# One Hyena layer with a SwiGLU feed-forward on one core: the element work of GpSimd goes to VectorE, and parts of VectorE's work go to ScalarE and to adding DMAs

## The chip, the core and the metric

The kernel runs on one core of one Trainium2 chip. The metric is the time of one execution on the device, in microseconds. A core has TensorE (PE in the profile: matmuls, and PEld for their weight loads), VectorE (DVE), ScalarE (ACT), GpSimd (POOL) and SyncE (SP). Each engine works through its own list of instructions in a fixed order; semaphores are all that ties the lists together. DMAs are issued here by SyncE (plain loads and stores) and by GpSimd (DMAs that add what they carry to what stands at the destination, and some stores).

## The reference

The model has one layer: `x + hyena(rmsnorm(x))`, then `x + swiglu(rmsnorm(x))`, then a last rmsnorm. Sequence and width are both 1024, the feed-forward is 2816 wide, all in float32. The mixer is what matters here:

```python
z = short_conv(u @ w_in + b_in, conv_w, conv_b)     # width 3, per channel
x0, x1, v = jnp.split(z, 3, axis=-1)
s = v * x1
g = hyena_filter(L, ...)                            # (2L, D), made by a small MLP
g = g / jnp.sum(jnp.abs(g), axis=0, keepdims=True)
y = irfft(rfft(s, n=2*L, axis=0) * rfft(g, n=2*L, axis=0), n=2*L, axis=0)[:L]
y = (y + s * skip) * x0
return y @ w_out + b_out
```

## The kernel before

The 1024 channels are cut into eight blocks of 128 (i = 0 to 7). Channels lie along the partitions for the projections, and the 1024 positions along the free dimension, in the order "residue mod 8, then the rest". The work runs in this order.

**Prologue.** rmsnorm and transposes of x, the MLP of the filter, and the projections of block 0.

**Hyena blocks**, the loop at line 483. For each block:

- `inproj` (L111, tiles `z`) makes one projection of 128 channels: 48 matmuls of 512 columns, because each float32 product is made of three products of a high and a low part. A block needs three: v, x1 and x0. `load_w_in` makes the low part of a weight with `split_dma`: ScalarE writes the high part (L120) and its negative (L121), and GpSimd issues a DMA that adds the raw weight (L122).
- `short_conv` (L310) takes a projection from PSUM to SBUF with the width-3 convolution: one ScalarE pass (L312), four VectorE passes that multiply and add (L319: two of 896 columns, two of 127) and a VectorE add of two columns for the edges (L320).
- `conv_vx` multiplies v and x1 to the signal s (L417, on GpSimd).
- `filter_g` makes the filter's taps (`ph` matmuls, `hw`), their L1 norm (L395, one VectorE reduction over absolute values) and their spectrum `gg`. `forward` transposes s (`pst`), and makes its spectrum `ss` (`pp` matmuls). Both end in `from_psum` (L360 ScalarE, L361 and L362 VectorE) and `butterfly` (L336 to L352): a small FFT of twelve additions and two multiply-adds. The butterfly of `gg` runs on GpSimd except for L352, that of `ss` on VectorE.
- `pointwise` multiplies the two spectra (L446 to L449 on GpSimd, L450 on VectorE; all on VectorE for block 7). `inverse` (L454, L455 and a butterfly, on VectorE) makes `vv`, and `finish` the result: `py` matmuls, L470 (ScalarE), L471 (VectorE) and the product with x0 (L472, on GpSimd for blocks 0 to 5), then a store to DRAM.

The blocks are run into one another: while block i is finished, the filter, the projections and the forward transform of block i+1 are under way. A scheduler of the framework fixes the order on each engine from its own estimate of times; the source's order gives priorities only. PSUM has two tiles `mm` (projections) and two tiles `cv` (all others). Tiles of SBUF are named by slot: `gg0` and `gg1` hold the filter's spectrum in turn, `ss` and `cr` the signal's spectrum and products, `ct_g` and `ct_d` the scratch of the two butterflies.

**Output projection** (`po`, L566), rmsnorm, and then the **feed-forward**: gate and up products (L714) and the down product (L944), both by a seven-product scheme for 2x2 blocks. In these stages the change edits nothing.

Of the kernel before, what the change touches and what calls it, by code (L numbers as in the profile page):

```python
# [73 lines left out]
def hyena_ffn_kernel(ctx: ExitStack, tc: tile.TileContext, a: dict, out: bass.AP):  # L74
# [280 lines left out]

    def from_psum(pts, E, o, nm):
        av, bv = ab_tiles(E, nm)
        for r in range(2):
# [2 lines left out]
            V.tensor_tensor(ar, pts[r][:, 0:512], br, ALU.add)  # L361
            V.tensor_tensor(br, pts[r][:, 0:512], br, ALU.subtract)  # L362
        butterfly(E, av, bv, o, nm)

    last_load = [None]

    def filter_g(i):
# [27 lines left out]
        V.tensor_reduce(  # L395
            l1, hw.rearrange("p j h c -> p c (j h)"), AX.X, ALU.add, apply_absolute_value=True
        )
        pts = []
        for r in range(2):
# [6 lines left out]
            pts.append(pt)  # L406
        gg = slot(f"gg{i % 2}", f"gg{i}", (2, NB, P))
        from_psum(pts, G, gg, f"g{i}")
        return gg, l1

    def conv_vx(i, pv, px):
        vz = slot("vz", f"vz{i}")
        short_conv(pv, vz, 16 + i)
# [4 lines left out]
        return s

    def conv_x0(i):  # L420
        x0 = slot("x0" if i < NB - 1 else "vz", f"x0{i}")
        short_conv(inproj(i), x0, i)
        return x0

    def forward(i, s):
        pst = cv_psum(f"pst{i}")
        for j in range(NB):
            T.transpose(pst[:, j * P : (j + 1) * P], s[:, j * P : (j + 1) * P], ident)
# [1 line left out]
        S.copy(sT.rearrange("p j c -> p (j c)"), pst)  # L430
        pts = []
        for r in range(2):
            pt = cv_psum(f"pp{i}_{r}")
            for j in range(NB):
                T.matmul(
                    pt[:, j * P : (j + 1) * P], fwd[r][:, j, :], sT[:, j, :], start=True, stop=True
                )
# [4 lines left out]

    def pointwise(i, ss, gg):
        cr = slot("cr" if i < NB - 1 else "ss", f"cr{i}", (2, NB, P))
        E = G if i < NB - 1 else V
        E.tensor_tensor(cr[:, 0], ss[:, 0], gg[:, 1], ALU.mult)  # L446
# [1 line left out]
        E.tensor_tensor(gg, ss, gg, ALU.mult)
        E.tensor_tensor(ss[:, 0], cr[:, 0], cr[:, 1], ALU.add)  # L449
        V.tensor_tensor(ss[:, 1], gg[:, 0], gg[:, 1], ALU.subtract)  # L450

    def inverse(i, ss):
# [1 line left out]
        V.tensor_tensor(av, ss[:, :, 0:4], ss[:, :, 4:8], ALU.add)  # L454
# [4 lines left out]

    def finish(i, vv, s, l1, x0):  # L460
# [10 lines left out]
        V.scalar_tensor_tensor(s, py, rn, s, ALU.mult, ALU.add)  # L471
# [598 lines left out]
```

## Time and profile before

| what | value |
|---|---|
| runs | 1278.81, 1277.39, 1271.57 us; median 1277.39 |
| the profiled execution | 1272.72 us, of which the span of instructions is 1271.0 us |
| TensorE busy in the span | 1181.9 us (93%) |
| VectorE | 922.4 us (73%) |
| ScalarE | 459.4 us (36%) |
| GpSimd | 334.1 us (26%) |
| mean granted TensorE clock | 0.976 |

The same execution by stage (busy us of each engine; the first column is the stretch in us from the span's start):

| stretch | what runs there | TensorE | VectorE | ScalarE | GpSimd |
|---|---|---|---|---|---|
| 0 to 40 | loads, norm, transposes | 18.77 | 23.43 | 23.88 | 3.07 |
| 40 to 120 | first projections, MLP of the filter | 77.72 | 42.58 | 35.33 | 18.94 |
| 120 to 480 | Hyena blocks | 325.03 | 343.74 | 114.76 | 219.50 |
| 480 to 560 | end of block 7, output projection | 75.51 | 48.86 | 32.32 | 8.79 |
| 560 to 640 | output projection, norm, first gate products | 70.86 | 57.78 | 35.76 | 24.39 |
| 640 to 1020 | gate and up products | 379.43 | 242.34 | 114.02 | 38.76 |
| 1020 to 1080 | turn to the down product | 52.17 | 35.42 | 18.90 | 4.24 |
| 1080 to 1271 | down product, last norm | 182.43 | 128.21 | 84.49 | 16.44 |

A row of the profile's timeline reads: start in us, length in us, engine, line, operation, tile written <- tiles read, shapes, count, and in brackets how long the engine had been idle and what ended that. A row of the groups by line reads: line, engine, operation, names, shapes, count | busy us, mean ns of one | idle time before them and what ended it. A row of the waits reads: who <- for whom: us in total, times, longest. A row of the stretches gives busy us and count for PE, PEld, DVE, ACT and POOL, then the granted TensorE clock, the share of the DMA engines and GB/s.

### The profile page before, as it was taken

The numbers are of one execution on the slowest core, as the hardware profiler recorded it, in microseconds if no ns is written. First come the engines' busy times: TensorE is split into PE (matmuls) and PEld (weight loads), VectorE is DVE, ScalarE is ACT, GpSimd is POOL, SyncE is SP. The second block draws the span as 40 slices with busy tenths as digits, with TensorE's granted clock in tenths as the row PEclk, the third lists the DMA queues.
The fourth block names the chain that finished last, engine by engine and source line by source line (L and its number), as shares of the span: only waits on it lengthen the run. The fifth ranks groups of instructions, "written<-read, shape, count | busy, mean of one in ns | idle before, by whom it ended". The sixth has DMA issues, their size and how long they took to land.

```text
span 1271.0 us, 15010 instructions
## 1 busy us (share of the span) xinstructions
PE 1181.9 (93%) x5678; PEld 979.9 (77%) x5678; DVE 922.4 (73%) x1363; ACT 459.4 (36%) x718; POOL 334.1 (26%) x322
## 2 busy tenths in 40 slices
PE   3899978799899798998899999999999998999997
PEld 3678867788788687876678888888888876888885
DVE  6555999899999999456865676666666647955675
ACT  6435323324143134434423332323332323334444
POOL 0024666548646652113310111100111110011100
PEclk9999989999899999999899999999999998999999
DMA  9635545222222329822131332322323259833333
GB/s 282 150 89 120 124 87 137 59 62 63 67 61 73 100 83 274 240 78 72 58 103 57 123 116 92 124 93 75 122 89 119 75 176 342 317 100 91 92 92 132
DMA packets 93993, 152.82 MB, mean 120 GB/s; under 512 B 7135, under 2 KB 58463, under 8 KB 93793
## 3 DMA queue, kind: packets, MB, share of 16 engines
q1 hardware_dynamic: 76241, 91.30, 21.8%
q0 software_dynamic: 17680, 60.57, 18.6%
q8 instruction: 44, 0.72, 0.2%
q14 instruction: 28, 0.23, 0.1%
HBM read 102.30 MB, written 40.11 MB: 112 GB/s over the span
## 4 chain that ended last, share of the span: by engine, by line
PE 63%; DVE 25%; DMA 6%; ACT 3%; issue 2%; POOL 1%; SPq 0%; ACTq 0%; DVEq 0%; POOLq 0%
PE bx L944 9%; PE z L111 7%; PE po L566 5%; PE by L944 5%; PE bz L944 2%; DVE l L395 2%; DVE ss L450 1%; DMA dc<-in_hy_decay_dram 1%; DVE vz L319 1%; DVE fwl L378 1%; DMA xt<-in_x_dram 1%; PE wu3dc L714 1%; PE wg1dc L714 1%; PE wu8dc L714 1%; PE wg5dc L714 1%
## 5 line engine op out<-in xcount | busy, mean ns | idle before, releaser
L111 PE MATMUL z<-uh,whl 128*128 128x512 f32 x768 | 222.4, 403 | 7.9 <-DVE x L319 2.8
L111 PEld LDWEIGHTS z<-uh,whl 128*128 128x128 f32 x768 | 145.5, 192 | 40.7 <-ACT uh L100 3.1
L111 PE MATMUL z<-ul,whl 128*128 128x512 f32 x384 | 128.8, 405 | 0.0
L944 PE MATMUL bx<-wop,hop 128*128 128x512 f32 x504 | 120.2, 399 | 5.6 <-ACT wop L100 4.0
L944 PEld LDWEIGHTS bx<-wop,hop 128*128 128x128 f32 x504 | 96.5, 192 | 28.2 <-ACT wop L100 4.5
L561 POOL DMA_DIRECT2D hd<-g x40 | 21.6, 542 | 330.6 <-DVE g L860 167.2
L566 PE MATMUL po<-wohl,uh 128*128 128x512 f32 x256 | 83.4, 408 | 6.6 <-ACT uh L100 3.7
L101 DVE TENSOR_TENSOR hop<-hrp,hop 128x1024 fp32r<-128x1024 f32 (+1 forms) x41 | 46.3, 1130 | 54.6 <-ACT hop L100 54.6
L111 PEld LDWEIGHTS z<-ul,whl 128*128 128x128 f32 x384 | 73.6, 193 | 15.6 <-issue 0.5
L100 ACT CAST hop<-hrp 128x1024 fp32r<-128x1024 f32 (+1 forms) x41 | 40.0, 977 | 104.3 <-PE bx L944 62.0
L561 POOL DMA_DIRECT2D hrp<-hd x42 | 22.3, 530 | 195.4 <-DVE hop L101 181.8
L566 PEld LDWEIGHTS po<-wohl,uh 128*128 128x128 f32 x256 | 49.0, 194 | 19.3 <-ACT uh L100 4.2
L944 PE MATMUL by<-wop,hop 128*128 128x512 f32 x264 | 60.8, 391 | 0.0
L944 PEld LDWEIGHTS by<-wop,hop 128*128 128x128 f32 x264 | 49.6, 188 | 10.9
L405 PE MATMUL pg<-hw,fwd 128*128 128x128 f32 x256 | 49.6, 277 | 7.9 <-DVE hw L393 7.2
L101 DVE TENSOR_TENSOR wop<-wd,wop 128x512 fp32r<-128x512 f32 x75 | 49.3, 684 | 4.5 <-ACT wop L100 4.5
L566 PE MATMUL po<-wohl,ul 128*128 128x512 f32 x128 | 51.4, 406 | 0.0
L404 PE MATMUL pg<-hw,fwd 128*128 128x128 f32 x256 | 49.7, 276 | 0.0
L100 ACT CAST wop<-wd 128x512 fp32r<-128x512 f32 x75 | 43.2, 616 | 14.7 <-PE by L944 11.9
L122 POOL DMA_DIRECT2D whl<-wt x24 | 22.5, 937 | 98.6 <-ACT whl L121 87.2
L405 PEld LDWEIGHTS pg<-hw,fwd 128*128 128x128 f32 x256 | 39.4, 193 | 8.8 <-DVE hw L393 7.4
L120 ACT CAST whl<-wt 128x1024 fp32r<-128x1024 f32 x24 | 25.0, 1043 | 49.8 <-DMA wt<-in_hy_w_in_dram 26.8
(1720 smaller groups left out, 2968.5 us busy)
## 6 DMA issues: line engine op xcount, KB each, us to landing
hrp<-hd POOLq DMA_DIRECT2D x35, 512.0 KB, 3.9
wt<-in_hy_w_in_dram SPq DMA_DIRECT2D x24, 512.0 KB
whl<-wt POOLq DMA_DIRECT2D x24, 512.0 KB, 4.6
wgr<-in_ffn_w_gate_dram SPq DMA_DIRECT2D x22, 512.0 KB
wur<-in_ffn_w_up_dram SPq DMA_DIRECT2D x22, 512.0 KB
wd<-in_ffn_w_down_dram SPq DMA_DIRECT2D x44, 256.0 KB
hd<-g POOLq DMA_DIRECT2D x40, 256.0 KB, 2.7
hd<-sx POOLq DMA_DIRECT2D x30, 256.0 KB, 2.8
```

The lines of the kernel that those rows point to most:

```text
L100: S.copy(hi, src)
L101: (eng or V).tensor_tensor(lo, src, hi.bitcast(F32), ALU.subtract)
L111: T.matmul(pt[:, h * 512 : (h + 1) * 512], w[wi], u2[ui][h][:, k, :], start=first and ti == 0, stop=last and ti == len(TERMS) - 1,)
L120: S.copy(hi, src)
L122: G.dma_start(lo.bitcast(F32), src, accum_op=ALU.add)
L395: V.tensor_reduce(l1, hw.rearrange("p j h c -> p c (j h)"), AX.X, ALU.add, apply_absolute_value=True)
L404: T.matmul(o, fwd[r][:, j, :], hw[:, j, 0, :], start=True, stop=False)
L405: T.matmul(o, fwd[2 * r][:, jj, :], hw[:, jj, 1, :], start=False, stop=True)
L561: G.dma_start(dst, src)
L566: T.matmul(o, u2[yi][th][:, k, m * P : (m + 1) * P], wos[h][k // 2][wi][:, k % 2, :], start=(k == 0 and ti == 0), stop=(k == NB - 1 and ti ...
L714: T.matmul(pt, t[:, wi, k, :], b(k)[ui], start=first and k == 0 and ti == 0, stop=k == 3 and ti == len(TERMS) - 1, skip_group_check=not first,
L944: T.matmul(pt, ho[hi_][:, x, q * P : (q + 1) * P], wo_[wi][:, x, :], start=fresh and first and x == 0 and ti == 0, stop=last and x == n - ...
```

## The change

In the Hyena blocks:

- **No element work on GpSimd.** The butterfly of `gg`, the product s, the products of the spectra and the product with x0 all go to VectorE. GpSimd only issues DMAs there.
- **Short convolution of v, and of x0 for blocks 0 to 5**: `short_conv_dma`. ScalarE writes the middle tap to z and the two other taps to a tile `taps` (six passes more, two of them of one column), and two GpSimd DMAs add `taps` to z. x1, and x0 of blocks 6 and 7, keep `short_conv`.
- **Pointwise product.** VectorE writes both products with the real part at once (L466, 2048 columns, one operand read twice by a stride of zero), then two products of 1024 columns into `ss` (L467, L468, one with a factor of -1). A GpSimd DMA of 1 MB adds `ss` to `cr` (L470); for block 7 VectorE adds. The result is now `cr`.
- **L1 norm**: ScalarE takes absolute values in three passes, VectorE adds in five steps, in place of one reduction.
- **Low part of the filter's weights** (`fwl`): by `split_dma` in place of a VectorE subtraction.
- **One spectrum buffer**: `gg` always lies in `gg0`; `gg1` holds `taps`. The slots of `ss` and `cr` swap for blocks 6 and 7.

```diff
+    def short_conv_dma(pt, z, n):
+        w0, w1_, w2_ = (cols[:, 24 + 24 * i + n : 25 + 24 * i + n] for i in range(3))
+        taps = slot("gg1", f"taps{n}", (2, 1024))
+        S.activation(z, pt, AF.Identity, bias=beta[:, n : n + 1], scale=w1_)
+        S.activation(taps[:, 0, 128:1024], pt[:, 0:896], AF.Copy, scale=w0)
+        S.activation(taps[:, 0, 1:128], pt[:, 896:1023], AF.Copy, scale=w0)
+        S.copy(taps[:, 0, 0:1], edge[:, n, 0:1])
+        G.dma_start(z, taps[:, 0], accum_op=ALU.add)
+        S.activation(taps[:, 1, 0:896], pt[:, 128:1024], AF.Copy, scale=w2_)
+        S.activation(taps[:, 1, 896:1023], pt[:, 1:128], AF.Copy, scale=w2_)
+        S.copy(taps[:, 1, 1023:1024], edge[:, n, 1:2])
+        G.dma_start(z, taps[:, 1], accum_op=ALU.add)
...
-    def butterfly(E, av, bv, o, nm, packed=False):
+    def butterfly(av, bv, o, nm, packed=False):
+        E = V
...
-        S.copy(fwh, fw)
-        V.tensor_tensor(fwl, fw, fwh.bitcast(F32), ALU.subtract)
+        split_dma(fwh, fwl, fw)
...
-        V.tensor_reduce(
-            l1, hw.rearrange("p j h c -> p c (j h)"), AX.X, ALU.add, apply_absolute_value=True
-        )
+        ma = slot("ct_g", f"ma{i}")
+        hf = hw.rearrange("p j h c -> p (j h c)")
+        S.activation(ma, hf[:, 0:1024], AF.Abs)
+        V.tensor_tensor(ma[:, 0:512], ma[:, 0:512], ma[:, 512:1024], ALU.add)
+        for q in (2, 3):
+            S.activation(ma[:, 512:1024], hf[:, q * 512 : (q + 1) * 512], AF.Abs)
+            V.tensor_tensor(ma[:, 0:512], ma[:, 0:512], ma[:, 512:1024], ALU.add)
+        V.tensor_tensor(ma[:, 0:256], ma[:, 0:256], ma[:, 256:512], ALU.add)
+        V.tensor_tensor(l1, ma[:, 0:128], ma[:, 128:256], ALU.add)
...
-        gg = slot(f"gg{i % 2}", f"gg{i}", (2, NB, P))
-        from_psum(pts, G, gg, f"g{i}")
+        gg = slot("gg0", f"gg{i}", (2, NB, P))
+        from_psum(pts, "ab_g", gg, f"g{i}")
...
-        short_conv(pv, vz, 16 + i)
+        short_conv_dma(pv, vz, 16 + i)
...
-        G.tensor_tensor(s, vz, xz, ALU.mult)
+        V.tensor_tensor(s, vz, xz, ALU.mult)
...
-        short_conv(inproj(i), x0, i)
+        (short_conv_dma if i < NB - 2 else short_conv)(inproj(i), x0, i)
...
-        E = G if i < NB - 1 else V
-        E.tensor_tensor(cr[:, 0], ss[:, 0], gg[:, 1], ALU.mult)
-        E.tensor_tensor(cr[:, 1], ss[:, 1], gg[:, 0], ALU.mult)
-        E.tensor_tensor(gg, ss, gg, ALU.mult)
-        E.tensor_tensor(ss[:, 0], cr[:, 0], cr[:, 1], ALU.add)
-        V.tensor_tensor(ss[:, 1], gg[:, 0], gg[:, 1], ALU.subtract)
+        V.tensor_tensor(cr, ss[:, 0:1].broadcast_to([P, 2, NB, P]), gg[:, ::-1], ALU.mult)
+        V.tensor_tensor(ss[:, 0], ss[:, 1], gg[:, 0], ALU.mult)
+        V.scalar_tensor_tensor(ss[:, 1], ss[:, 1], -1.0, gg[:, 1], ALU.mult, ALU.mult)
+        if i < NB - 1:
+            G.dma_start(cr, ss, accum_op=ALU.add)
+        else:
+            V.tensor_tensor(cr, cr, ss, ALU.add)
+        return cr
...
-        (G if i < NB - 2 else V).tensor_tensor(s, s, x0, ALU.mult)
+        V.tensor_tensor(s, s, x0, ALU.mult)
```

Lines up to 320 keep their numbers; later ones are higher in the changed kernel (L454 becomes L477, L361 becomes L375). `taps` is one slot for v and x0, so ScalarE's writes to it wait until the adds of the taps before have landed. The edits also make the scheduler place instructions anew, in the Hyena blocks above all.

GpSimd's order around the products of block 5, before (`ss5`, `gg5`, `cr5` are the spectra of block 5, `sig4` is s of block 4, `g6` the butterfly of the next filter, `whl` the weights of a projection):

```order
L446 TENSOR_TENSOR cr5_2590<-ss5_2542,gg5_2298 128x1024 [waits DVE_49,PE_49,Pool_49]
L447 TENSOR_TENSOR cr5_2590<-ss5_2542,gg5_2298 128x1024
L472 TENSOR_TENSOR sig4_2056<-sig4_2056,x04_2451 128x1024 [waits DVE_49]
L448 TENSOR_TENSOR gg5_2298<-ss5_2542,gg5_2298 128x2048 [waits Pool_49]
L122 DMA whl23_3086<-wt23_3084 128x1024 [waits DMASW2_49,DMAHW5_49,PE_49,Activation_49]
L449 TENSOR_TENSOR ss5_2542<-cr5_2590 128x1024 [waits Pool_49]
L417 TENSOR_TENSOR sig6_2838<-vz6_2824,xz6_2831 128x1024 [waits DMAHW6_49,DVE_49]
L336 TENSOR_TENSOR g6ct_2699<-g6ab_2692 128x512 [waits DVE_49]
```

And now (DMASW names the semaphore of a DMA that GpSimd issued):

```order
L333 DMA x04_2540<-taps4_2596 128x1024 [waits DMASW2_49]
L329 DMA vz6_2925<-taps22_2926 128x1024 [waits DMASW6_49,DVE_49,Activation_49]
L333 DMA vz6_2925<-taps22_2926 128x1024 [waits DMASW6_49,Activation_49]
L122 DMA whl5_2948<-wt5_2946 128x1024 [waits DMASW0_49,DMAHW4_49,PE_49,Activation_49]
L122 DMA whl23_3203<-wt23_3201 128x1024 [waits DMASW1_49,DMAHW5_49,PE_49,Activation_49]
L122 DMA whl15_3258<-wt15_3256 128x1024 [waits DMASW0_49,DMAHW6_49,PE_49,Activation_49]
L329 DMA x05_2945<-taps5_3001 128x1024 [waits DMASW3_49,DMASW5_49,DVE_49,Activation_49]
L470 DMA cr5_2683<-ss5_2635 128x2048 [waits DMASW4_49,DVE_49]
L333 DMA x05_2945<-taps5_3001 128x1024 [waits DMASW3_49,Activation_49]
```

The element work is gone from GpSimd's list, and the low parts of the weights (L122) stand behind the tap adds, of which the second (L333) waits for the first (L329) to land.

VectorE's order from the products to the inverse transform of block 4, before:

```order
L450 TENSOR_TENSOR ss4_2149<-gg4_1905 128x1024 [waits Pool_49]
L361 TENSOR_TENSOR g5ab_2299<-pg5_0_2264,g5ab_2299 128x512 [waits Activation_49]
L362 TENSOR_TENSOR g5ab_2299<-pg5_0_2264,g5ab_2299 128x512 [waits DVE_49]
L454 TENSOR_TENSOR y4ab_2203<-ss4_2149 128x1024 [waits Pool_49]
L455 TENSOR_TENSOR y4ab_2203<-ss4_2149 128x1024
```

And now the same place of block 5 (`ma6` is the L1 norm of the next filter, `sig6` the next s, `hw6` the next taps):

```order
L466 TENSOR_TENSOR cr5_2683<-ss5_2635,gg5_2383 128x2048 [waits DVE_49]
L495 TENSOR_TENSOR sig4_2129<-sig4_2129,x04_2540 128x1024 [waits DMASW5_49,DVE_49]
L406 MEMSET hw6_2718 1x128 [waits DVE_49]
L467 TENSOR_TENSOR ss5_2635<-ss5_2635,gg5_2383 128x1024 [waits DVE_49]
L405 TENSOR_TENSOR hw6_2718<-ph6_1_2737,hw6_2718 128x1024 [waits PE_49]
L468 SCALAR_TENSOR_TENSOR ss5_2635<-ss5_2635,gg5_2383 128x1024 [waits DVE_49]
L436 TENSOR_TENSOR sig6_2943<-vz6_2925,xz6_2936 128x1024 [waits DMAHW7_49,DMASW7_49]
L411 TENSOR_TENSOR ma6_2749<-ma6_2749 128x512 [waits Activation_49]
L414 TENSOR_TENSOR ma6_2749<-ma6_2749 128x512 [waits Activation_49] x2
L415 TENSOR_TENSOR ma6_2749<-ma6_2749 128x256 [waits DVE_49]
L477 TENSOR_TENSOR y5ab_2688<-cr5_2683 128x1024 [waits DMASW4_49]
L478 TENSOR_TENSOR y5ab_2688<-cr5_2683 128x1024
```

Between the last product (L468), which lets the 1 MB add go, and L477, which waits for that add, stand five VectorE instructions.

More of the change, by code (lines that the diff above doesn't have):

```diff
@@ L320, in short_conv, with ab_tiles @@
         V.tensor_tensor(z[:, 0:1024:1023], z[:, 0:1024:1023], edge[:, n, :], ALU.add)
-    def ab_tiles(E, nm):
-        ab = slot("ab_g" if E is G else "ab_d", nm + "ab", (2, 2, 4, P))
+    def short_conv_dma(pt, z, n):
[10 more added lines that the diff above has]
+        G.dma_start(z, taps[:, 1], accum_op=ALU.add)
+    def ab_tiles(which, nm):
+        ab = slot(which, nm + "ab", (2, 2, 4, P))
         return ab[:, 0], ab[:, 1]
-    def butterfly(E, av, bv, o, nm, packed=False):
+    def butterfly(av, bv, o, nm, packed=False):
+        E = V
         a23 = av[:, :, 3:1:-1] if packed else av[:, :, 2:4]
@@ L332, in butterfly @@
         bf = bv.rearrange("p r q c -> p (r q) c")
-        ct = slot("ct_g" if E is G else "ct_d", nm + "ct", (8, P))
+        ct = slot("ct_d", nm + "ct", (8, P))
         cc = ct[:, 0:4].rearrange("p (r q) c -> p r q c", r=2)
@@ L354, in butterfly, with from_psum @@
             )
-    def from_psum(pts, E, o, nm):
-        av, bv = ab_tiles(E, nm)
+    def from_psum(pts, which, o, nm):
+        av, bv = ab_tiles(which, nm)
         for r in range(2):
@@ L362, in from_psum @@
             V.tensor_tensor(br, pts[r][:, 0:512], br, ALU.subtract)
-        butterfly(E, av, bv, o, nm)
+        butterfly(av, bv, o, nm)
     last_load = [None]
@@ L421, in conv_x0 @@
         x0 = slot("x0" if i < NB - 1 else "vz", f"x0{i}")
-        short_conv(inproj(i), x0, i)
+        (short_conv_dma if i < NB - 2 else short_conv)(inproj(i), x0, i)
         return x0
+    SPEC = [("ss", "cr")] * (NB - 2) + [("cr", "ss"), ("hw", "ss")]
     def forward(i, s):
@@ L438, in forward @@
             pts.append(pt)
-        ss = slot("ss" if i < NB - 1 else "hw", f"ss{i}", (2, NB, P))
-        from_psum(pts, V, ss, f"s{i}")
+        ss = slot(SPEC[i][0], f"ss{i}", (2, NB, P))
+        from_psum(pts, "ab_d", ss, f"s{i}")
         return ss
     def pointwise(i, ss, gg):
-        cr = slot("cr" if i < NB - 1 else "ss", f"cr{i}", (2, NB, P))
-        E = G if i < NB - 1 else V
-        E.tensor_tensor(cr[:, 0], ss[:, 0], gg[:, 1], ALU.mult)
-        E.tensor_tensor(cr[:, 1], ss[:, 1], gg[:, 0], ALU.mult)
-        E.tensor_tensor(gg, ss, gg, ALU.mult)
-        E.tensor_tensor(ss[:, 0], cr[:, 0], cr[:, 1], ALU.add)
-        V.tensor_tensor(ss[:, 1], gg[:, 0], gg[:, 1], ALU.subtract)
+        cr = slot(SPEC[i][1], f"cr{i}", (2, NB, P))
+        V.tensor_tensor(cr, ss[:, 0:1].broadcast_to([P, 2, NB, P]), gg[:, ::-1], ALU.mult)
[6 more added lines that the diff above has]
+        return cr
     def inverse(i, ss):
-        av, bv = ab_tiles(V, f"y{i}")
+        av, bv = ab_tiles("ab_d", f"y{i}")
         V.tensor_tensor(av, ss[:, :, 0:4], ss[:, :, 4:8], ALU.add)
         V.tensor_tensor(bv, ss[:, :, 0:4], ss[:, :, 4:8], ALU.subtract)
-        vv = slot("cr" if i < NB - 1 else "ss", f"vv{i}", (2, NB, P))
-        butterfly(V, av, bv, vv, f"y{i}", packed=True)
+        vv = slot(SPEC[i][0], f"vv{i}", (2, NB, P))
+        butterfly(av, bv, vv, f"y{i}", packed=True)
         return vv
@@ L480, in hyena_ffn_kernel @@
     ss = forward(0, s)
-    pointwise(0, ss, gg)
+    ss = pointwise(0, ss, gg)
     vv = inverse(0, ss)
@@ L492, in hyena_ffn_kernel @@
             ss1 = forward(i + 1, s1)
-            pointwise(i + 1, ss1, gg)
+            ss1 = pointwise(i + 1, ss1, gg)
         x0 = conv_x0(i)
@@ L500, in hyena_ffn_kernel @@
         if not last:
-            pointwise(i + 1, ss1, gg)
+            ss1 = pointwise(i + 1, ss1, gg)
         if i < NB - 3 or last:
```

## Prediction

> **What bounds the kernel now.** I read the stretches first, then what TensorE waits for, then single instructions on VectorE and GpSimd. The stretch of the Hyena blocks:
>
> ```profile
> 120.00:480.00 360.00, 325.03 (x1910) 284.55 (x1910) 343.74 (x428) 114.76 (x164) 219.50 (x152) 0.96 0.35 85
> ```
>
> TensorE is idle 35.0 of 360 us, its granted clock is 0.96, and VectorE is busy for 95% of the time; in the table by stage, the gate and up products leave TensorE idle for 0.6 of 380 us. The waits of TensorE in that stretch, the longest:
>
> ```profile
> PE pg L405 <- DVE hw L393: 7.2, 1, 7.2
> PE pst L428 <- DVE g3ab L362: 6.6, 1, 6.6
> PE pn L462 <- DVE s1ab L362: 5.9, 1, 5.9
> PE pn L462 <- DVE s4ab L362: 4.2, 1, 4.2
> PE pn L462 <- DVE s2ab L362: 4.1, 1, 4.1
> ```
>
> 28.0 of the 35.0 us, all on VectorE: it is late, and TensorE, with work for most of the time, stands behind it. Why VectorE is so full is seen in its own rows, here beside one of GpSimd (timeline; the first is GpSimd's):
>
> ```profile
> 141.16 4.82 POOL L448 TENSOR_TENSOR gg<-ss,gg 128x2048 f32<-128x2048 f32 x1
> ```
> ```profile
> 142.67 3.34 DVE L320 TENSOR_TENSOR xz<-xz,edge 128x2 f32<-128x2 f32 x1
> 150.79 1.82 DVE L454 TENSOR_TENSOR y0ab<-ss 128x1024 f32<-128x1024 f32 x1
> 165.92 1.29 DVE L352 SCALAR_TENSOR_TENSOR vv<-y0ab 128x512 f32<-128x512 f32 x2
> 499.63 0.15 DVE L320 TENSOR_TENSOR x<-x,edge 128x2 f32<-128x2 f32 x1
> 506.63 1.22 DVE L454 TENSOR_TENSOR y7ab<-ss 128x1024 f32<-128x1024 f32 x1
> 509.51 0.41 DVE L338 TENSOR_TENSOR y7ct<-y7ab 128x256 f32<-128x256 f32 x1
> 513.58 1.29 DVE L352 SCALAR_TENSOR_TENSOR vv<-y7ab 128x512 f32<-128x512 f32 x2
> ```
>
> An add of two columns takes 0.15 us alone, and 3.34 us when it starts inside GpSimd's L448: it ends when that ends (141.16 + 4.82 = 145.98; 142.67 + 3.34 = 146.01). The inverse transform of block 0, beside GpSimd's butterfly, takes 165.92 + 1.29 - 150.79 = 16.4 us; that of block 7, when GpSimd has no element work, 8.2 us (506.63 to 514.87), instruction for instruction the same. So much of VectorE's time is waiting inside its instructions for GpSimd.
>
> **The length of a block.** The transposed signal is copied once a block:
>
> ```profile
> L430 ACT COPY sT<-pst x8: 989/1002/1017, 115.2 to 469.0; 128x1024 f32<-128x1024 f32 x8
> ```
>
> (469.0 - 115.2) / 7 = 50.5 us a block; the stretch of 360 us holds 7.1. Per block VectorE is busy 343.74 / 7.1 = 48.2 us, TensorE 45.6 us, of which up to 0.04 x 50.5 = 2.0 are its slower clock.
>
> **VectorE after, per block.** Its operations at their lengths without GpSimd's element work:
>
> ```profile
> 102.91 2.96 DVE L319 SCALAR_TENSOR_TENSOR x<-z,cols,x 128x896 f32<-128x896 f32 x4
> 131.80 2.34 DVE L392 TENSOR_TENSOR hw<-ph,hw 128x1024 f32<-128x1024 f32 x2
> 182.83 3.77 DVE L395 TENSOR_REDUCE l<-hw 128x128 f32<-128x2048 f32 x1
> 482.39 0.68 DVE L361 TENSOR_TENSOR s7ab<-pp,s7ab 128x512 f32<-128x512 f32 x1
> 493.68 1.27 DVE L471 SCALAR_TENSOR_TENSOR sig<-py,rn,sig 128x1024 f32<-128x1024 f32 x1
> 496.76 1.22 DVE L446 TENSOR_TENSOR cr<-ss,gg 128x1024 f32<-128x1024 f32 x1
> 500.84 2.28 DVE L448 TENSOR_TENSOR gg<-ss,gg 128x2048 f32<-128x2048 f32 x1
> ```
>
> The inverse of 8.2 us begins with two additions of 1.1 (1.22, but instructions overlap by some 0.08), so a butterfly with its two multiply-adds is 6.0 us; the four PSUM adds (L361's kind) are 0.6 each. So: s 8.4, filter spectrum 8.4 (before 2.4 + 1.3, the rest on GpSimd), inverse 8.2, one short convolution 3.1 (before three, 9.3), taps 2.5, L1 norm 3 x 0.6 + 0.6 = 2.4 (before 3.8), products of the spectra 2.28 + 1.22 + 1.27 = 4.8 (before 1.2), s product, L471 and x0 product 1.22 + 1.27 + 1.22 and a reciprocal = 3.9 (before 1.4), low part of the filter weights none (before 0.4). Sum after 41.7. The same sum before is 38.9, against 48.2 busy: 9.3 us a block go in waits for GpSimd, some 66 us in the stretch. The change adds 2.8 us of work to VectorE and takes those 9.3 away: 48.2 to 41.7.
>
> **What the new waits cost.** VectorE now stands in its list at L477 until the 1 MB add has landed. From issue to landing, by the DMA groups:
>
> ```profile
> whl<-wt POOLq DMA_DIRECT2D x24, 512.0 KB, 4.6
> ...
> hd<-g POOLq DMA_DIRECT2D x40, 256.0 KB, 2.7
> ...
> hrp<-hd POOLq DMA_DIRECT2D x35, 512.0 KB, 3.9
> ...
> ul<-yr POOLq DMA_DIRECT2D x6, 256.0 KB, 10.0
> ```
>
> `whl` is the same kind, an add from SBUF to SBUF. 1 MB is not in the trace. Below it is bounded by 4.6; above by 10.0, adds of 256 KB that were issued in a crowd. From 256 to 512 KB is 1.2 us, so I take 4.6 + 2.4 = 7.0, near the lower end, since these adds stand apart from each other. Between L468 and L477 VectorE has five instructions, 1.2 + 3 x 0.6 + 0.3 = 3.3 us: it stalls 3.7 us a block, between 1.3 and 6.7. Behind L477 stands the inverse and then the filter's butterfly; for `py`, which reads the inverse's `vv`, TensorE has from `pg` on 88 projection matmuls, `pst` and `pp` to do first, 25 us at the rates below, so 3.7 us there cost nothing but VectorE's own time. VectorE's block: 41.7 + 3.7 = 45.4.
>
> The tap adds are in series: 2.7 us of ScalarE (1.2 and 1.4, rows below), 4.6, then 4.6 again: v is ready 12 us after its projection, x0 too. s is needed a whole block later, x0 as well: nothing on the path. Behind the second tap add stands `whl` of the x0 projection; it lands some 13 us after v's projection ends. TensorE comes to it after 48 matmuls of x1 (less those done), `pst` and `pp`:
>
> ```profile
> 155.02 3.73 PE L435 MATMUL pp<-sT,fwd 128*128 128x128 f32 x32
> ...
> 158.82 1.09 PE L111 MATMUL z<-uh,whl 128*128 128x512 f32 x4
> ```
>
> 48 x 0.229 + 0.9 + 3.6 = 15.5 us: 2.5 us to spare. If that is gone, TensorE waits for the excess in each block.
>
> ScalarE has 114.76 / 7.1 = 16.1 us a block. It gains two sets of taps and absolute values:
>
> ```profile
> L121 ACT ACTIVATE whl<-whl 128x1024 fp32r<-128x1024 f32 x17 | 18.0, 1057 | 0.4
> ...
> L312 ACT ACTIVATE vz<-z,beta,cols 128x1024 f32<-128x1024 f32 x6 | 7.2, 1199 | 3.5 <-PE z L111 3.5
> ```
>
> At about 1.0 for 896 columns, 0.3 for 127, 0.2 for one, two taps are 3.0, twice 6.0; absolute values 1.1 + 2 x 0.6; 0.4 for `fwl`: 8.7 us, to 25 of some 46. It hides, and it now frees the PSUM of v and x0 itself, without VectorE. The single `gg` buffer costs nothing: VectorE reads it in L468 and writes it later in the same list. `fwl` is added 20 us ahead of its matmuls.
>
> **A rule against the change.** GpSimd's issue beside VectorE's additions of SBUF data:
>
> ```profile
> 278.75 0.87 POOL L122 DMA_DIRECT2D whl<-wt  x1 [8.46 <-ACT whl L121]
> 278.95 0.41 DVE L346 TENSOR_TENSOR ss<-s3ct 128x256 f32<-128x256 f32 x1
> ```
>
> Beside the issue the addition of 256 columns takes the 0.41 us that it takes alone (509.51, above), so I add nothing for the six issues more a block. The Trainium skill, "SBUF — State Buffer", section "SBUF: two separate sides", warns that a DMA issued by GpSimd stalls while VectorE runs an operation that holds both its port pairs, since GpSimd cannot write the descriptors; the rows above do not show it for these additions. If it held here, an issue could wait for the longest of them, 2.28 us, and the landing be 6.9 in place of 4.6: the case of the half gain below.
>
> **TensorE after.** After a wait its matmuls run at half pace:
>
> ```profile
> 221.37 0.63 PE L468 MATMUL py<-inv,vv 128*128 128x128 f32 x2
> ...
> 224.42 0.39 PE L468 MATMUL py<-inv,vv 128*128 128x128 f32 x2
> ```
>
> 0.63 us for a pair against 0.39, three microseconds later. So a wait that goes takes its slow clock with it: the stretch can lose 35.0 of idle time and up to 0.04 x 360 = 14 of slow clock, 49 us at most. The Trainium skill, "TensorE: Matmul & The Clock Gate", Part 1, has the clock halved after an idle window of about 3.4 us and freed after as long a busy one. By that, waits shortened below 3.4 us would cost no clock at all, and the sum would keep the whole 14; the rows agree, with waits of 4.1 us ahead of the slow pairs.
>
> **The sum.** TensorE needs 45.6 - 2.0 = 43.6 to 45.6 us a block, VectorE 45.4 with its stall; both lists are fixed and wait for each other here and there. I take 45.8 for a block: 4.7 x 7.1 = 33.5 us of 1272.72, the profiled execution (1271.0 of span and 1.7 around it): 1239.2. The other stages have the same work. The median of the runs, 1277.39, is 4.7 above the profiled execution; the forecast for a median is 1277.4 - 33.5 = 1243.9, say 1244.
>
> **Rivals.** *Half the gain:* the adds land in 6.6 us or more in place of 4.6. Then `whl` uses up its 2.5 us (two adds in series and its own make 3 x 2 = 6 more: 3.5 us of wait on TensorE), and a block is some 48.5: 2.0 x 7.1 = 14 us, 1263. For it: the add queue holds six more DMAs a block. Against: the DMA engines are busy 0.35 of the time. Chance 0.14.
>
> *Slower:* adds at the 10.0 us of the crowded row. ScalarE, before it writes the taps of x0, waits for both adds of v: 2.7 + 20 = 23 us after v's projection, and behind that wait in its list stand the PSUM copies of `pp`, which are due at 16. All of VectorE's s stage comes 7 us late, of which it has some 3 to spare before `py`; the 1 MB add costs 3 more. 45.8 + 4 + 3 = 52.8 us, and with `whl` late too 54: 3.5 x 7.1 = 25 us above, 1302. It decides from 2.7 + 2 x 6.6 = 16 us on. Chance 0.06.
>
> *Not what it says:* VectorE's long rows have another cause and stay. Then 41.7 + 9.3 = 51.0, some 0.5 to 1 us a block above now: 1277 to 1284. Against it stands the pair 16.4 and 8.2 us. Chance 0.03.
>
> **How the numbers follow.** The forecast has 0.77, from 1229 (all 49 us) to 1256. Half the gain reaches from there to 1272. The range 1229 to 1265 leaves out the slower cases and the end of the half gain. A measurement of this kernel can tell about 0.5%, 6.4 us, from no change: faster takes the forecast and most of the half gain, 0.88; same 0.06; slower 0.06.
>
> **What would show it.** Right: VectorE busy some 300 us in the Hyena blocks, its inverse at 8.2 us in every block, no edge add over 0.2 us, a step of the copies of sT near 45 us, TensorE idle under 15 us there. L477 waits 2 to 5 us for `cr`. Wrong: TensorE waiting for `whl`, ScalarE at the column copies of `taps` with PSUM copies late behind it, landings of the adds over 6.6 us, or VectorE's additions as long as before.

## The result and the profile after

The changed kernel takes 1322.22 us (median of four runs, 1318.93 to 1322.99) against 1276.41 of the kernel before (the three runs of the table above and one more): a ratio of 1.0359, interval 1.0323 to 1.0395. It is slower by 3.6%, where the forecast was 1244 us and the range ended at 1265. The profiled execution has a span of 1316.9 us, 45.9 more than before.

The span is cut at the last copy of the transposed signal (block 7, ScalarE), which the forecast used too:

```profile
L451 ACT COPY sT<-pst x8: 987/1014/1036, 112.4 to 495.7; 128x1024 f32<-128x1024 f32 x8
```

Before, it started at 469.0. So the Hyena blocks end 26.7 us later, and what follows takes 1316.9 - 495.7 = 821.2 us in place of 1271.0 - 469.0 = 802.0, 19.2 more. There are two losses, in two places.

The stretch of the Hyena blocks, with the columns of the table of before:

```profile
120.00:480.00 360.00, 321.70 (x1799) 278.53 (x1798) 258.76 (x455) 146.11 (x238) 49.01 (x57) 0.94 0.63 135
```

VectorE is busy for 258.76 us in place of 343.74, but TensorE, which should have filled up, is idle for 38.3 us (before 35.0), at a granted clock of 0.94 (0.96). What TensorE waits for from 120 to 525 us, and ScalarE's longest waits in the same window:

```profile
PE z L111 <- DMA whl<-wt: 24.3, 6, 5.2
PE po L589 <- ACT wohl L100: 7.5, 1, 7.5
PE pn L485 <- DVE s2ab L376: 4.0, 1, 4.0
```
```profile
ACT whl L120 <- PE z L111: 54.3, 5, 11.5
ACT taps L328 <- DMA x<-taps: 43.8, 5, 14.1
...
ACT taps L328 <- DMA vz<-taps: 26.0, 5, 8.3
```

The waits for VectorE's filter and norm work have shrunk; the weights' low parts (`whl`) have come in their place, six waits of up to 5.2 us. ScalarE stands 69.8 us at L328, a copy of one column. The add queue in block 3 (GpSimd's timeline; `x<-taps` are the taps of x0), and ScalarE's rows of the same time:

```profile
308.41 0.86 POOL L329 DMA_DIRECT2D x<-taps  x1 [3.30 <-ACT taps L327]
309.52 0.86 POOL L470 DMA_DIRECT2D cr<-ss  x1 [0.25 <-DVE ss L468]
311.25 0.86 POOL L122 DMA_DIRECT2D fwl<-fw  x1 [0.87 <-ACT fwl L121]
314.89 0.86 POOL L333 DMA_DIRECT2D x<-taps  x1 [2.77 <-DVE ma L414]
...
335.38 0.86 POOL L333 DMA_DIRECT2D vz<-taps  x1 [4.54 <-ACT whl L121]
335.96 1.17 POOL L122 DMA_DIRECT2D whl<-wt  x1
```
```profile
323.48 0.19 ACT L328 COPY taps<-edge 128x1 f32<-128x1 f32 x1 [7.16 <-DMA x<-taps]
...
323.67 0.58 ACT L374 COPY g4ab<-pg 128x512 f32<-128x512 f32 x1
324.14 3.31 ACT L395 ACTIVATE hw<-dc,negt 128x256 f32<-128x256 f32 x8
327.35 1.19 ACT L325 ACTIVATE vz<-z,beta,cols 128x1024 f32<-128x1024 f32 x1
...
330.72 1.05 ACT L120 CAST whl<-wt 128x1024 fp32r<-128x1024 f32 x1
...
333.92 1.06 ACT L121 ACTIVATE whl<-whl 128x1024 fp32r<-128x1024 f32 x1
```

This is the loss of one block, read backward. TensorE needs `whl` at 337.9. Its add was issued at 335.96, since ScalarE wrote the negative high part only at 333.92, and right behind v's second tap add (335.38), which had waited for v's first one, issued at 329.98, to land; with that add beside it `whl` took 6.5 us. Both stand behind ScalarE's list. ScalarE was late because from 316 to 323.48 it had stood at the column copy of the **next** taps (v's), which reads only `edge`, stands ahead of v's other passes (from 327.35) in its list, and may not write into `taps` until both adds of x0's taps have landed. Those take from 308.41 to 323.40: the 1 MB add and `fwl` are between them in the same queue.

Four of the six waits for `whl` (17.5 of the 24.3 us) come about like this one. In the first two, of 4.31 and 2.50 us, `whl` itself landed late, 12.2 and 10.1 us after its issue, beside adds of the output bias that the kernel before has too.

The adds by group:

```profile
whl<-wt POOLq DMA_DIRECT2D x24, 512.0 KB, 5.4
...
vz<-taps POOLq DMA_DIRECT2D x16, 512.0 KB, 4.6
...
cr<-ss POOLq DMA_DIRECT2D x7, 1024.0 KB, 11.3
x<-taps POOLq DMA_DIRECT2D x12, 512.0 KB, 7.5
```

And TensorE behind its wait (timeline): four matmuls of 512 columns take 2.07 and 1.89 us, where they take 1.08 elsewhere, so this wait costs about 2 us more. The Trainium skill, "TensorE: Matmul & The Clock Gate", Part 1, has the clock halved after some 3.4 us of idle time; the wait of 4.67 us agrees.

```profile
342.55 2.07 PE L111 MATMUL z<-uh,whl 128*128 128x512 f32 x4 [4.67 <-DMA whl<-wt]
344.42 1.05 PE L111 MATMUL z<-ul,whl 128*128 128x512 f32 x2
345.28 1.89 PE L111 MATMUL z<-uh,whl 128*128 128x512 f32 x4
```

The second loss is at the turn to the output projection. TensorE's longest waits from 480 to 640 us (`wohl` are the high and low parts of the output weights), and ScalarE's row that ends the first:

```profile
PE po L589 <- ACT wohl L120: 10.5, 1, 10.5
PE po L589 <- DMA wohl<-wo: 9.3, 1, 9.3
PE po L589 <- ACT wohl L100: 7.5, 1, 7.5
```
```profile
532.70 1.04 ACT L120 CAST wohl<-wo 128x1024 fp32r<-128x1024 f32 x1 [1.74 <-DVE ss L468]
```

The second piece of the output weights lies in the slot `gg0`. Before, `gg0` was free by then, as the last filter's spectrum lay in `gg1`; now every spectrum lies in `gg0`, and ScalarE may write there only after the last product of block 7 (L468). The wait of 10.5 us and the 9.3 us for the add behind it are this piece. In this row ScalarE waits only 1.74 us for L468, and before it 8.8 us for the load of another piece, so the trace alone does not say how much of them is the slot's; swap_gg, below, does.

### The profile page after: what moved, and what is told of

Read it like the earlier page. It is cut to its first block, busy times and chain, and to the rows that moved or that the text cites. A ratio compares the mean times of both kernels' runs of the same rounds, so it can differ in the third digit from the quotient of the medians.

```text
span 1316.9 us, 15156 instructions
## 1 busy us (share of the span) xinstructions
PE 1193.6 (91%) x5678; PEld 987.2 (75%) x5678; DVE 862.3 (65%) x1440; ACT 512.2 (39%) x834; POOL 162.0 (12%) x227
## 4 chain that ended last, share of the span: by engine, by line
PE 59%; DMA 14%; DVE 8%; ACT 5%; issue 4%; POOL 0%; SPq 0%; POOLq 0%; ACTq 0%; DVEq 0%
PE bx L967 8%; PE po L589 5%; PE z L111 5%; PE by L967 4%; DMA x<-taps 4%; DMA vz<-taps 3%; DMA whl<-wt 3%; PE bz L967 2%; PE py L491 1%; PE py L492 1%; ACT hw L395 1%; DMA cr<-ss 1%; PE wu3dc L737 1%; PE wg1dc L737 1%; PE wu8dc L737 1%
## 5 line engine op out<-in xcount | busy, mean ns | idle before, releaser
L111 PE MATMUL z<-uh,whl 128*128 128x512 f32 x768 | 228.6, 412 | 32.3 <-DMA whl<-wt 28.8
L111 PEld LDWEIGHTS z<-uh,whl 128*128 128x128 f32 x768 | 148.3, 197 | 66.6 <-DMA whl<-wt 31.6
L589 PE MATMUL po<-wohl,uh 128*128 128x512 f32 x256 | 88.0, 425 | 29.5 <-ACT wohl L120 10.5
L589 PEld LDWEIGHTS po<-wohl,uh 128*128 128x128 f32 x256 | 51.0, 203 | 43.7 <-ACT wohl L120 10.6
L967 PEld LDWEIGHTS by<-wop,hop 128*128 128x128 f32 x264 | 49.6, 188 | 10.8
L101 DVE TENSOR_TENSOR wop<-wd,wop 128x512 fp32r<-128x512 f32 x75 | 49.2, 686 | 5.7 <-ACT wop L100 5.7
L122 POOL DMA_DIRECT2D whl<-wt x24 | 23.1, 961 | 172.4 <-ACT whl L121 163.4
```

The costliest lines, as they stand in the source:

```text
L101: (eng or V).tensor_tensor(lo, src, hi.bitcast(F32), ALU.subtract)
L111: T.matmul(pt[:, h * 512 : (h + 1) * 512], w[wi], u2[ui][h][:, k, :], start=first and ti == 0, stop=last and ti == len(TERMS) - 1,)
L122: G.dma_start(lo.bitcast(F32), src, accum_op=ALU.add)
L589: T.matmul(o, u2[yi][th][:, k, m * P : (m + 1) * P], wos[h][k // 2][wi][:, k % 2, :], start=(k == 0 and ti == 0), stop=(k == NB - 1 and ti ...
L967: T.matmul(pt, ho[hi_][:, x, q * P : (q + 1) * P], wo_[wi][:, x, :], start=fresh and first and x == 0 and ti == 0, stop=last and x == n - ...
```

## The experiments

All times are medians; ratios are to the kernel before, with their intervals. The profiles of all are cut as above: start of the last copy of sT, and time from there to the end. The kernel before was run again beside each group: its median was 1276.4 to 1277.2 us beside the kernels down to x0_col_swap and 1274.7 or 1274.9 beside those from x0_s7v on, so kernels of different groups are best compared by their ratios. A profile is one execution, up to 7 us from its kernel's median (x0_swap's is 6.8 above), so a few us in the last two columns mean little. Each edit also lets the scheduler place instructions anew.

| kernel | median us | ratio | last sT | from there |
|---|---|---|---|---|
| before | | 1 | 469.0 | 802.0 |
| changed | 1322.2 | 1.0359 [1.0323, 1.0395] | 495.7 | 821.2 |
| col_late | 1294.1 | 1.0148 [1.0111, 1.0185] | 467.0 | 828.4 |
| cr_dve | 1291.8 | 1.0131 [1.0090, 1.0173] | 464.0 | 823.9 |
| x0_dve | 1278.5 | 1.0023 [1.0004, 1.0042] | 452.4 | 823.5 |
| all_dve | 1289.5 | 1.0108 [1.0061, 1.0155] | 463.5 | 825.3 |
| swap_gg | 1309.8 | 1.0268 [1.0229, 1.0307] | 501.6 | 806.3 |
| x0_swap | 1264.4 | 0.9910 [0.9882, 0.9938] | 454.2 | 815.2 |
| all_swap | 1270.7 | 0.9956 [0.9936, 0.9976] | 463.8 | 802.6 |
| x0_col_swap | 1264.4 | 0.9906 [0.9874, 0.9939] | 454.9 | 808.7 |
| x0_s7v | 1260.7 | 0.9888 [0.9851, 0.9926] | 454.7 | 808.7 |
| x0_gpool | 1288.1 | 1.0124 [1.0084, 1.0164] | 484.9 | 800.2 |
| cr_only_swap | 1253.8 | 0.9848 [0.9816, 0.9881] | 452.9 | 802.4 |
| v_only_swap | 1257.0 | 0.9874 [0.9843, 0.9904] | 461.2 | 796.9 |
| col_swap | 1280.3 | 1.0034 [1.0016, 1.0053] | 469.4 | 809.1 |
| col_cr_swap | 1261.1 | 0.9887 [0.9864, 0.9910] | 462.6 | 796.4 |

**col_late: the columns behind the projection.**

```diff
-        S.copy(taps[:, 0, 0:1], edge[:, n, 0:1])
+        S.activation(taps[:, 0, 0:1], pt[:, 0:1], AF.Identity, bias=edge[:, n, 0:1], scale=0.0)
...
-        S.copy(taps[:, 1, 1023:1024], edge[:, n, 1:2])
+        S.activation(taps[:, 1, 1023:1024], pt[:, 0:1], AF.Identity, bias=edge[:, n, 1:2], scale=0.0)
```

> Theory A: ScalarE is held at the head of its list. The two column copies of taps (L328, L332) read only the edges, so they stand far ahead of the projection they belong to, and wait there until both adds of the taps before have landed (69.8 us in the changed kernel, up to 14.1 at once); PSUM copies, exponentials and the high parts of the next weights stand behind them, and TensorE then waits for whl (24.3 us). Here the two columns are written by a pass that also reads the projection (times zero), so they can only stand behind it; work and DMAs are the same. A expects ScalarE's waits for the adds under 15 us, TensorE's waits for whl under 8, the step from one pg to the next 57.5 -> 51 us, the whole 1322 -> about 1285. Theory B: the add queue itself is too slow (1 MB in 11 us, the taps of x0 in 7.5 us twice), and the wait only shows it: it moves to L326, and the time stays within 1310 to 1322. Theory C: VectorE's longer list sets the block: no change, 1318 to 1325.

1294.1 us, 28 less, with the same work and the same adds. ScalarE's waits for adds of taps from 120 to 525 us, 69.8 us in the changed kernel, and all of TensorE's from 80 to 460:

```profile
ACT taps L326 <- DMA x<-taps: 8.1, 5, 2.4
```
```profile
PE pp L456 <- ACT sT L451: 9.7, 3, 4.1
PE z L111 <- DMA whl<-wt: 6.1, 1, 6.1
```

Theory A holds: with the copies of 0.19 us moved back in ScalarE's list, 28 us are gone. They are those of the whole edit: the scheduler also placed other instructions of ScalarE and VectorE anew. C falls, and B as the sole cause. What A missed is the turn, 828.4 us as before.

**cr_dve: no 1 MB add.**

```diff
-        if i < NB - 1:
-            G.dma_start(cr, ss, accum_op=ALU.add)
-        else:
-            V.tensor_tensor(cr, cr, ss, ALU.add)
+        V.tensor_tensor(cr, cr, ss, ALU.add)
```

> The pointwise sum by VectorE in every block (2.3 us), no 1 MB add. Theory B (the add queue): the two adds of the taps of x0, 15 us from the first issue to the last landing with the 1 MB add between them, take 10; the stalls at L477 (5 to 6.5 us a block) go; 5 us less a block, about 1290. Theory A: the wait of ScalarE at the early column copies gets shorter by the same 5 us but stays (about 40 of 70 us left): 1295 to 1305. Theory C (VectorE's list): 2.3 us more a block, 5 less of stall: within 10 us of the changed kernel.

1291.8. x0's adds now land in 5.6 us in place of 7.5, and ScalarE's waits at L328 fall from 69.8 to 49.8 us. The time lies between what B and A gave, and the run does not tell them apart; C falls, as the kernel with 2.3 us more of VectorE work a block is 30 us faster.

**x0_dve: x0's short convolution by VectorE.**

```diff
-        (short_conv_dma if i < NB - 2 else short_conv)(inproj(i), x0, i)
+        short_conv(inproj(i), x0, i)
```

> The short convolution of x0 by VectorE in every block (3.1 us more), that of v still by adds, the 1 MB add stays. Theory A: the early column copies now wait only for the adds of v of the block before, which landed long ago; ScalarE's waits at L328 go, 1285 to 1295. Theory B: half of the traffic of the taps goes, the 1 MB add lands in 7 us; 1290 to 1300. Theory C: 3.1 us more of VectorE a block, slower: 1330 to 1340.

1278.5, 44 less: more than either theory gave. L328 still waits, 29.2 us for v's adds, but they cost nothing that shows: x0_col_swap, below, takes such waits away and is no faster. The last copy of sT starts at 452.4, 16.6 us earlier than in the kernel before; 21.5 us of that are given back at the turn.

**all_dve: only the move from GpSimd** (the edits of cr_dve and x0_dve, and `short_conv` for v).

> Only the move from GpSimd: short convolutions and the pointwise sum all on VectorE, no adding DMAs but the weights' low parts. VectorE's work per block is 41.7 + 6.2 + 2.3 = 50 us without stalls, as long as a block of before (50.5) with TensorE's 46 beside it. Theories A and B: no waits for adds are left, so the block is 50 to 52 and the time 1270 to 1295. Theory C (the order of VectorE's list, with the butterfly of the filter in it, sets the block): 57 or more, 1320 to 1340.

1289.5: blocks of 49.8 us ((463.5 - 115.0) / 7), 5.5 us earlier at the last copy, and the turn 23.3 us longer. A and B were right on the blocks. The turn is lost in all four kernels alike, so it does not hang on the adds.

**swap_gg: the two slots exchanged.**

```diff
-        taps = slot("gg1", f"taps{n}", (2, 1024))
+        taps = slot("gg0", f"taps{n}", (2, 1024))
...
-        gg = slot("gg0", f"gg{i}", (2, NB, P))
+        gg = slot("gg1", f"gg{i}", (2, NB, P))
```

> The changed kernel with the two slots exchanged: taps in gg0, the one spectrum buffer in gg1. Nothing else is edited. The turn to the output projection: its second piece of weights (wohl01) lies in gg0, which in the changed kernel holds the last filter's spectrum until the last product of block 7 (L468); ScalarE waits for that (L120 <- L468), TensorE waits 10.5 us for ScalarE and 9.3 us for the add behind it. Theory T (the slot's next tenant): those two waits of 20 us go, with the clock behind them, and the time falls from 1322 to about 1300, while the blocks (last copy of sT at 495.7) stay as late. Rival U: the loads of y and of the weights are late by themselves (SyncE takes 18 us for five of them), the waits move to the next pieces; 1315 to 1322.

1309.8, 12 less. VectorE's and ScalarE's lists stay nearly as they were in the blocks. The waits for the second piece are gone; of TensorE's waits for output weights one is left (490 to 650 us):

```profile
PE po L589 <- ACT wohl L100: 7.9, 1, 7.9
```

Theory T holds, at 12 in place of 20 us: the part behind the last copy is 14.9 us shorter, the blocks end 5.9 us later in this profile.

**x0_swap, all_swap, x0_col_swap: the exchange with the earlier edits.**

> Short convolution of x0 on VectorE (as in x0_dve, 1278) and the slots exchanged. In x0_dve the last projection ends at 449.7 us (before: 484.2), and 36 us are lost at the turn. Theory T: 20 to 30 of them come back, 1250 to 1258, and this beats the kernel before by 1.5 to 2%. Rival U: 1270 to 1278.

> Only the move from GpSimd to VectorE (as in all_dve, 1289) and the slots exchanged. Theory T: 1262 to 1270, so that the move by itself, with 50 us of VectorE work per block, is worth 5 to 15 us. Rival U: 1282 to 1289.

> As x0_swap, and the columns of v's taps written behind the projection (as in col_late). ScalarE's waits at the early columns (29 us in x0_dve) go too. In x0_dve TensorE was busy 248.8 of 250 us in the blocks, so I expect no gain in the steady blocks: within 5 us of x0_swap. If ScalarE's waits still cost something, it is 5 to 15 us faster.

The exchange is worth 14 us with x0_dve (1264.4) and 19 with all_dve (1270.7); both now beat the kernel before. Less came back than the 20 to 30 expected of x0_swap, and all_swap lies just above its range of 1262 to 1270. x0_col_swap, in which ScalarE's waits at the early columns (28.8 us in x0_swap) are gone, is no faster than x0_swap, as expected where TensorE is full. TensorE's rows for 190 to 440 us, of x0_swap and of the kernel before:

```profile
190.00:440.00 250.00, 249.57 (x1480) 219.54 (x1481) 219.00 (x389) 110.80 (x170) 31.32 (x37) 1.00 0.59 132
```
```profile
190.00:440.00 250.00, 228.56 (x1319) 198.97 (x1319) 237.18 (x301) 77.48 (x111) 148.16 (x104) 0.97 0.31 73
```

This is what the forecast had foreseen: VectorE no longer late, TensorE busy 249.57 of 250 us at full clock. But the copies of sT come every 49.2 us there ((409.2 - 212.3) / 4), not every 45.8.

**x0_s7v: block 7's spectrum out of PSUM by VectorE.**

```diff
-            S.copy(br, pts[r][:, 512:1024])
+            (V.tensor_copy if nm == "s7" else S.copy)(br, pts[r][:, 512:1024])
```

> x0_swap (1264), and for block 7 alone the two copies of the signal's spectrum out of PSUM (L374, s7) by VectorE. In x0_swap they stand in ScalarE's list behind a cast of the output weights that waits until 482.7 us for its load; pp7 was done at 461, so the last block loses 22 us there, and what the blocks gained (last projection at 449 against 484 us) is gone at the turn. Theory L (the turn is a chain of latencies behind ScalarE's list): VectorE is free for them from 475, 9 us earlier, and the time falls by 8 to 12 us to about 1254. Rival (the loads of the output weights set the turn): the wait moves there, 1260 to 1265.

1260.7, 3.7 less, which the intervals do not tell from nothing. The copies moved from 483.6 to 474.8 as planned, and TensorE still waits 9.0 us for the first piece of the output weights. The rival was nearer.

**x0_gpool: GpSimd gets the filter's butterfly back.**

```diff
-        E = V
+        E = G if nm[0] == "g" else V
...
-        ct = slot("ct_d", nm + "ct", (8, P))
+        ct = slot("ct_g" if E is G else "ct_d", nm + "ct", (8, P))
```

> x0_swap (1264) with the twelve additions of the filter's butterfly back on GpSimd, which in the kernel before were the largest piece of its element work. Contention theory: VectorE has 4.8 us less work a block, but its instructions with two operands from SBUF take longer beside GpSimd's (an edge add over 0.5 us, the inverse over 10 us in place of 8.2); by the share of GpSimd's element work (12 of some 28 us a block before, for which VectorE paid 9.3) VectorE pays back 4 us, so its busy time in the blocks hardly falls, and the time is within 5 us of 1264. Rival (no contention, long rows had another cause): inverse 8.2 us, edge adds 0.15, VectorE's busy time 4.8 us a block less.

1288.1, 24 more than x0_swap (27 by the ratios), where I expected 5 at most. The stretches, then rows of VectorE and of GpSimd at the same time:

```profile
190.00:440.00 250.00, 235.29 (x1361) 204.77 (x1359) 197.90 (x297) 107.26 (x165) 89.25 (x93) 0.97 0.55 117
```
```profile
260.43 1.51 DVE L356 TENSOR_TENSOR y2ab<-y2ab 128x256 f32<-128x256 f32 x1
261.87 0.96 DVE L363 TENSOR_TENSOR vv<-y2ab 128x256 f32<-128x256 f32 x1
262.75 0.96 DVE L364 TENSOR_TENSOR vv<-y2ab 128x256 f32<-128x256 f32 x1
```
```profile
260.30 1.36 POOL L351 TENSOR_TENSOR g3ab<-g3ab 128x512 f32<-128x512 f32 x1
261.63 0.92 POOL L359 TENSOR_TENSOR gg<-g3ct 128x256 f32<-128x256 f32 x1
262.51 0.92 POOL L360 TENSOR_TENSOR gg<-g3ct 128x256 f32<-128x256 f32 x1
...
268.98 0.87 POOL L329 DMA_DIRECT2D vz<-taps  x1
```

VectorE's additions of 256 columns take 0.96 or 1.51 us in place of 0.42, in step with GpSimd's own. Its busy time a block is 197.90 / 250 x 55.3 = 43.8 us against 219.00 / 250 x 49.2 = 43.1 in x0_swap, though 4.8 us of work were taken off it: the contention is shown, and it eats the whole gain. Of its two signs that I had named, the inverse shows it (block 2: 15.0 us, in x0_swap 10.6, with other instructions in between), the edge adds hardly (one of eleven over 0.2 us). The Trainium skill, "SBUF — State Buffer", section "Who interferes with whom", has a VectorE instruction with two SBUF inputs contend with a GpSimd instruction that reads SBUF; these rows agree. The 24 us are not this alone: v's tap add (268.98) stands behind ten of GpSimd's additions, and TensorE waits 11.4 us for `whl` from 120 to 440 us (x0_swap 4.7). The two were not tried apart.

**cr_only_swap and v_only_swap: one kind of add at a time** (all_swap with the 1 MB add alone, and with v's taps alone).

> All short convolutions on VectorE, only the pointwise sum by the 1 MB add (all_swap, 1270.7, with that one add). VectorE has 2.3 us less work a block and a wait at L477. If the add, alone in its queue, lands in 7 us as I had estimated, VectorE stalls about as long as it saves: 1266 to 1274. If it lands in 10 us or more by itself: 1275 to 1285. If the stall lies where VectorE has time: 1256 to 1264.

> Only v's taps by adds; pointwise sum and x0 on VectorE (all_swap, 1270.7, with v's two adds; x0_swap, 1264, without the 1 MB add). VectorE's work is 47 us a block, without a stall at L477, against TensorE's 49.5 in the steady blocks: 1262 to 1268. If the 1 MB add had cost VectorE more than the 2.3 us that it saves, under 1262; if it was worth its stall, 1266 to 1271.

1253.8 and 1257.0. By the ratios they are 14 and 10 us faster than all_swap: each of the two adds pays alone. Against x0_swap, which has both, cr_only_swap is 8 us faster; v_only_swap's 5 us are not told from nothing by the intervals. Alone, the 1 MB add takes 8.0 us (7.2 to 10.3), and VectorE's stalls at L477 are 0.5 to 5.2 us: the third case of cr_only_swap, and a little more. v_only_swap, under 1262, is the case in which the 1 MB add costs more than the 2.3 us that it saves, but the profiles do not show this cost in the blocks: with that add beside v's taps the last copy of sT comes 7 us earlier (454.2 against 461.2), and the time is lost behind it (815.2 against 796.9). cr_only_swap is the fastest kernel here, 1.5% below the kernel before.

**col_swap and col_cr_swap: all adds, both mends; and the same without the 1 MB add.**

> The changed kernel with every one of its adds, and both mends: the columns of taps behind the projection (col_late, 28 us) and the two slots exchanged (swap_gg, 12 us). If the two causes are separate and between them the whole of what went wrong, 1322 - 28 - 12 = 1282 or, with the last projection at 464 us and a turn as in x0_swap, down to 1275. If the crowded adds (1 MB in 9.3 us, x0's taps in 6.5) cost more than that, it stays at 1285 to 1290, above the kernel before.

> As col_swap, but the pointwise sum by VectorE: the taps of v and x0 by adds, no 1 MB add, 2.3 us more of VectorE a block (44 in all, against TensorE's 49.5). If what is left in col_swap is the crowd in the add queue, 1258 to 1268. If it is the taps' adds by themselves (one slot, two adds in series, twice a block), no better than col_swap.

1280.3 is close to the sum, 1322 - 28 - 12 = 1282: the early columns and the slot are separate causes. All adds together then still cost 0.3% against the kernel before. Without the 1 MB add it is 1261.1: beside the taps of v and x0 that add costs 19 us, where alone it gained 14. In col_swap it takes 9.3 us and `whl` 6.6, where they take 8.0 in cr_only_swap and 4.6 in the kernel before. So the adds together are a third cause, but not all of the 19 us are shown to be the crowd in the queue: only 6.8 of them lie ahead of the last copy of sT (469.4 against 462.6). Some 10 more lie between it and the copies of block 7's spectrum out of PSUM, when no 1 MB add is under way. ScalarE's rows, first of col_swap, then of col_cr_swap:

```profile
496.94 1.04 ACT L120 CAST wohl<-wo 128x1024 fp32r<-128x1024 f32 x1 [11.22 <-DMA wo<-in_hy_w_out_dram]
497.90 1.07 ACT L374 COPY s7ab<-pp 128x512 f32<-128x512 f32 x2
```
```profile
481.03 1.08 ACT L374 COPY s7ab<-pp 128x512 f32<-128x512 f32 x2 [4.68 <-DVE vv L366]
```

In col_swap the scheduler put these copies behind a cast of the output weights that waits 11.2 us for its load, in col_cr_swap not. Taking them out from behind that cast was worth 3.7 us in x0_s7v, not told from nothing. How the 19 us divide between the queue and this order stays open.

| adds, besides the weights' (slots exchanged) | without the 1 MB add | with it |
|---|---|---|
| none | 1270.7 | 1253.8 |
| v's taps | 1257.0 | 1264.4 |
| v's and x0's taps, late columns | 1261.1 | 1280.3 |
| v's and x0's taps, as changed | not tried | 1309.8 |

## Why the prediction was wrong

- **VectorE's contention with GpSimd: right.** In the changed kernel no edge add from 120 to 440 us is over 0.16 us, and VectorE's work in one block (307 to 365 us) is 41.10 us; the sum had 41.7. The inverse of block 3 takes 10.8 us and not 8.2, because five instructions of the next filter stand in it; its own additions take 0.42 us for 256 columns, as when alone (0.41). x0_gpool brings the contention back.
- **"Some 300 us" of VectorE in the stretch: 258.76**, because the blocks are 57.5 us long, so that only 6.3 of them lie in it.
- **The stall at L477, 3.7 us (1.3 to 6.7): 4.9 to 6.5** for blocks 0 to 5. The 1 MB add landed in 11.3 us, above my upper bound of 10.0; "these adds stand apart from each other" was wrong, since VectorE's last product and x0's taps come at the same time in each block. VectorE had room for the stall: 41.10 us of work in 57.5. The rule against the change, that the issue itself stalls, is not what happened: the issues above take 0.86 to 1.17 us, and those of `whl` 0.96 us in the mean, before 0.94.
- **"The tap adds are in series ... nothing on the path": this step failed.** s and x0 were indeed not needed early. But `taps` is one slot, ScalarE is the engine that waits for it, and its list also holds the PSUM copies and the casts of the weights. 28 us by col_late, 44 by x0_dve, which takes the crowd away as well.
- **`whl` has 2.5 us to spare: no**, six waits, 24.3 us, and half pace behind the longer ones. I had it late behind slow tap adds; in four of the six ScalarE's list was late, for the cast of `whl` as for the taps ahead of it in the queue, and in two `whl` landed late beside other adds.
- **"The single `gg` buffer costs nothing": failed**, 12 to 19 us. I followed the buffer inside the loop and did not ask who has the slot next.
- **TensorE needs 43.6 to 45.6 us a block: mis-sized.** I divided the stretch's busy time by 7.1 blocks, but it holds 839 matmuls of projections, 118 a block, since some six of the 24 projections lie ahead of it. A full block has 144: 26 x 0.229 = 6 us more, 49.6, as x0_swap's 49.2 shows. So where TensorE was full, the last copy of sT came 16 us earlier (cr_only_swap: 452.9 against 469.0), and not 33.5. TensorE then finishes its last projection early, at 436.4 in place of 484.2 us, but has less to fill the chain of the last two blocks with: from 437 to 510 us it is busy for 56.68 of 73 us there, at a granted clock of 0.84, in the kernel before for 62.04, at 0.93.
- **The rivals.** "Slower" named the mechanism: ScalarE at the taps, PSUM copies and `whl` late behind it, from landings of 6.6 us on; x0's landed in 7.5. Its 0.06 and its 1302 were both too low. "Half the gain" had a slip in its sum: by the prediction's own 13 us, `whl` lands behind one tap add and its own, so that adds 2 us slower make it 4 us later, not 6, and TensorE's wait 1.5 us, not 3.5. "Slower" looked at v's adds ahead of x0's taps, and not at the place of the column copies in ScalarE's list, from which the wait for the adds starts as soon as the engine comes there.

## What to carry to other kernels

For each wait that a change adds, read the engine's list from the waiting instruction on: what stands behind it, and whether its place follows from data that are ready long before. Price a shared add queue by all that is issued into it at the same time, not by one transfer: here the 1 MB add and v's taps each paid alone (14 and 10 us), and with x0's taps all together lost, even with both mends. When a slot gets a new tenant or a longer one, look up its next tenant beyond the loop.

## What was not expected of the hardware

Adds from SBUF to SBUF that are in flight at once behave as if they shared a rate: the four of block 3 (512 KB, 1 MB, 128 KB, 512 KB) took from 308.41 to 323.40 us, some 150 KB per us, where 512 KB alone (v's taps) land in 4.6 us. The 1 MB add takes 8.0 (cr_only_swap), 8.5 (x0_swap), 9.3 (col_swap) or 11.3 us (the changed kernel; medians) by what else is in the queue at that time.
